# First norm's weight and bias: on VectorE ahead of the spill instead of mostly on GpSimd behind it; second gated unit's weights split ahead of that

## The chip, the cores and the metric

The kernel runs on one core of one Trainium2 chip. The metric is the device time of one execution in microseconds. Three runs of the kernel before give 1960.56, 1960.99 and 1962.79; the median is 1960.99.

## What is computed

One encoder layer over 1024 tokens of 1024 features in float32, with three sub-layers of the same outer form; a vector `c` gives each its shift, scale and gate. The last multiplication and addition of the layer norm, by `g` and `b`, are what the change moves, for the first sub-layer.

```python
def layer_norm(x, g, b):
    ...
    y = (xf - mu) * lax.rsqrt(var + LN_EPS)
    return (y * g.astype(jnp.float32) + b.astype(jnp.float32)).astype(x.dtype)

def post_norm_sublayer(x, mod, weight, f, g, b):
    shift, scale, gate = mod[:, 0, None, :], mod[:, 1, None, :], mod[:, 2, None, :]
    y = f(x * (1.0 + scale) + shift)
    return layer_norm(ALPHA * x + weight * (1.0 + gate) * y, g, b)

def swiglu(h, w_in, w_out):
    gate, up = jnp.split(h @ w_in, 2, axis=-1)
    return (jax.nn.silu(gate) * up) @ w_out

def hybrid_mixer(h, ...):
    proj = h @ w_in
    glu_a, glu_b, q, k, v = jnp.split(proj, ...)        # 512 columns each
    conv_out = conformer_conv(glu_a, glu_b, ...)        # u = glu_a * sigmoid(glu_b); depthwise, 31 wide; layer norm; silu
    attn_out = diff_attention(q, k, v, ...)             # two softmax maps per head, partial rotary on q and k
    return jnp.concatenate([conv_out, attn_out], axis=-1) @ w_out

    x = post_norm_sublayer(x, mod[:, 0], 0.5, swiglu 1, ln1_g, ln1_b)
    x = post_norm_sublayer(x, mod[:, 1], 1.0, hybrid_mixer, ln2_g, ln2_b)
    x = post_norm_sublayer(x, mod[:, 2], 0.5, swiglu 2, ln3_g, ln3_b)
```

## The kernel before

Tokens lie in eight tiles of 128 (`xt[t]`, one token per partition). Every matrix product is made from three: each operand is split into a rounded high part (a cast, `split`, L139, on ScalarE) and the rest (a subtraction, L140, on VectorE), and high by high, low by high and high by low are summed. The two SwiGLU products use the Strassen-Winograd form, with halves of the tokens and of the columns.

The stages follow each other in this way. SwiGLU 1 ends with `out_phase`, which calls `done(t)` for each finished token tile and `after(half, k)` for each feature tile of a half. `done` normalizes `xt[t]` without `g` and `b` (`norm_tile`, L257) and writes it to DRAM (`spill1[t]`, L883), from ScalarE's queue. `after` transposes the normalized tiles (`hT1`), and the mixer's features `hm` come from these with `g`, `b`, the shift and the scale folded into one scale and bias per feature (`A1`, `B1`): the mixer does not read `g` and `b` in token form. They are needed only in the residual of sub-layer 2.

The mixer's projections (pool `mproj`) come next. Four gated units of 128 columns each are made (`glu`, L913): unit `i` has weights loaded by `load_glu` in two halves (`glur`, from SP's queue), split into `gluh` and `glul`; `u` is the product of one part with the sigmoid of the other (`sg`, L920; `u`, L921). The weights of unit 0 are split early, in `done(4)`, into slots of a general heap. Then k, q and v are projected (`proj_tok`, L948 and L961), k and q get their rotary terms on GpSimd (L978 to L981). The depthwise convolution runs on VectorE (`cacc`, L926 and L932, 4 + 120 instructions), with a low priority, so that it fills the time between others. `ql` is the low part of the rotated queries (L1026 on VectorE, L1028 on GpSimd), transposed into `qT` by TensorE (L1040), and the scores (`sc`, L1055) follow, with their maxima on VectorE (`mx`, L1058).

After the attention of a tile, `finish(t)` scales it by the root of its squares' mean (`ss`, L1145, and a chain of small instructions on 128x4, L229 to L241, then L1149). The output projection (pool `p3a`) reads the normalized tiles back from DRAM into `x1[t]` (L1250, SP's queue), multiplies by `g` and adds `b` (`affine`, L266 and L267; tiles 0 to 5 on GpSimd, 6 and 7 on VectorE, by `XG`), and adds the products `mo` (L1293) of features `fh`, `fl` and weights `moh`, `mol` to it on VectorE (L1297 for the first quarter, L1299 behind it). What follows there is in an order given by a string (`MSEQ`).

The engines execute their own instructions in order. The order on each is made by a scheduler, from priorities that follow the code except where they are set by hand. SP's queue carries nearly all loads, in order: a DMA that waits keeps back all that stand behind it.

Of the kernel before, what the change touches and what calls it, by code (L numbers as in the profile page):

```python
# [17 lines left out]
NT = T // P  # L18
# [5 lines left out]
H = 512  # L24
# [12 lines left out]
XG = 6  # L37
# [13 lines left out]
def layer_kernel(ctx, tc, a, out):  # L51
# [227 lines left out]
    # Strassen-Winograd right operands of a pair of feature tiles (2 k, 2 k + 1); token halves are the columns.  # L279
    def right_first(name, ops, hb, eng=V):  # L280
        """hb: feature tiles 2 k and 2 k + 1 of token half 0."""
# [5 lines left out]
    def right_second(name, ops, hb, hc, eng=G, lo=V):  # L287
        """hc: feature tiles 2 k and 2 k + 1 of token half 1."""
# [35 lines left out]
    def in_tags(wp, order):  # L324
        """Has the tiles that are free first lie first."""
        for tag in order.split():
            shape, bufs = TAGS[tag]
            wp.tile(shape, F32, tag=tag, bufs=bufs, name=f"{tag}_")
# [43 lines left out]
    def product(ps, left, right, ks=range(4), more=False):  # L372
        """more: on top of the sum that the bank holds."""
# [11 lines left out]
    even = {}  # L385
# [6 lines left out]
    def in_steps(wp, s, j, L, ops, gd, begun={}):  # L392
        """The seven products of a pair of gate and up tiles; the left operands of the second half to DRAM."""
# [11 lines left out]
        def prod(left, right, ps=None):  # L405
            """ps: the bank that holds the sum so far."""
# [127 lines left out]
    # ---- SwiGLU, second half: product with w_out in Strassen-Winograd form (token halves, halves of the columns,  # L534
    # even and odd feature tiles), residual; done(t) follows each finished token tile; after(half, k) the tiles
    # of a half, some way into the next products ----
    def out_phase(s, wp, w_out, gd, gate, xs, done, after, hook):
# [6 lines left out]
        wa = {}  # L544
# [6 lines left out]
        def prep(n, k):  # L551
            """Operands of step k of product n; wa holds B11, then T1, and B22, wb B12, then T3, and B21, then T4."""
# [139 lines left out]
    # ================= sub-layer 1 =================  # L692
    x_in = a["x"][0]
    with pool("p1a") as wp:
# [27 lines left out]
        def first_mod(kk, raws, n):  # L722
            """The last n of its four blocks are summed on the vector engine first."""
# [47 lines left out]
        def early(wp, s, w_in, ops):  # L771
# [10 lines left out]
            # a: ada loads, x: token loads, w: weights, M: modulation, H: modulated features, R: right  # L782
            # operands, G and S: left operands, g: products; "d" has the vector engine take more of it
# [55 lines left out]
    with pool("p1b") as wp:  # L839
# [41 lines left out]
        def done(t):  # L881
            norm_tile(xt[t], f"1_{t}")
            S.dma_start(spill1[t], xt[t])  # L883
# [597 lines left out]
```

## Time and profile before

| | |
|---|---|
| median of three runs | 1960.99 us |
| span of the profiled execution (the page has no other time for it) | 1958.3 us |
| TensorE busy | 1832.7 us, 94% |
| VectorE busy | 1538.3 us, 79% |
| ScalarE busy | 781.3 us, 40% |
| GpSimd busy | 405.6 us, 21% |
| the twelve affine instructions on GpSimd | from 1131.65 to 1162.0 us |

The span is that of one execution; starts in the timelines are counted from its begin. Engines are named PE (TensorE matmuls), PEld (its weight loads), DVE (VectorE), ACT (ScalarE), POOL (GpSimd) and SP. Out and in of an instruction stand as `out<-in`, by the program's names without their numbers.

### The profile page before, as it was taken

Reading aid. Unit: us, or ns where it says so; the run is one execution under the profiler, and the core shown is the slowest. Engines: PE = TensorE matmul, PEld = TensorE weight load, DVE = VectorE, ACT = ScalarE, POOL = GpSimd, SP = SyncE. Lnnn points to the kernel's source line nnn. Section 1 sums busy time; section 2 is a strip of 40 time slices with the busy share of each in tenths; the row PEclk is TensorE's granted clock in tenths of the full one; section 3 lists DMA queues with packets and bytes.
Section 4 is the critical chain, followed back from the end, with each engine's and each line's share of the span. In section 5 each row is a group of like instructions: output and inputs, shape, how many; then the busy total and the mean of one; then the engine's idle time right before and its main releaser. Section 6 shows DMA issues by size and latency. Waiting matters only on the chain. (4 is left out here: it accounts for less than half of the span.)

```text
span 1958.3 us, 23453 instructions
## 1 busy us (share of the span) xinstructions
PE 1832.7 (94%) x8562; PEld 1514.4 (77%) x8562; DVE 1538.3 (79%) x2276; ACT 781.3 (40%) x1240; POOL 405.6 (21%) x280
## 2 busy tenths in 40 slices
PE   5899999999999999999999859989999999997896
PEld 4688888888888788888888748768888888885675
DVE  8867768675697978999689989896565756589888
ACT  3423333333445441142677642643333333443541
POOL 2200000000000020168476561430000000036034
PEclk7899999999999999999999879989999999998998
DMA  8527445533885322110000032234333432574511
GB/s 251 166 92 223 157 140 188 167 119 130 302 282 155 113 95 62 33 44 33 1 1 1 25 124 78 97 114 139 102 100 116 129 97 86 192 261 155 162 65 70
DMA packets 201394, 238.39 MB, mean 122 GB/s; under 512 B 13866, under 2 KB 124575, under 8 KB 201278
## 3 DMA queue, kind: packets, MB, share of 16 engines
q1 hardware_dynamic: 197786, 225.06, 35.7%
q0 software_dynamic: 2112, 7.34, 1.0%
q10 hardware_dynamic: 1380, 4.49, 0.6%
q8 instruction: 67, 1.10, 0.2%
q14 instruction: 49, 0.40, 0.1%
HBM read 183.89 MB, written 52.95 MB: 121 GB/s over the span
## 5 line engine op out<-in xcount | busy, mean ns | idle before, releaser
L589 PE MATMUL fo<-wr,gl 128*128 128x512 f32 x1848 | 430.4, 394 | 25.8 <-DVE wr L140 13.3
L589 PEld LDWEIGHTS fo<-wr,gl 128*128 128x128 f32 x1848 | 349.2, 190 | 105.0 <-DVE wr L140 16.0
L140 DVE TENSOR_TENSOR sl<-sf,sh 128x1024 fp32r<-128x1024 f32 x87 | 110.6, 1272 | 145.2 <-ACT sh L139 145.2
L139 ACT CAST sh<-sf 128x1024 fp32r<-128x1024 f32 x88 | 92.7, 1053 | 209.9 <-issue 31.5
L399 POOL DMA_DIRECT2D gd<-gf x8 | 4.5, 568 | 824.9 <-DVE gf L465 824.3
L932 DVE SCALAR_TENSOR_TENSOR cacc<-u,convw,cacc 128x1015 f32<-128x1015 f32 (+14 forms) x120 | 152.3, 1319 | 0.9
L140 DVE TENSOR_TENSOR gl<-gr,gl 128x512 fp32r<-128x512 f32 x148 | 110.6, 754 | 8.1 <-ACT gl L139 6.7
L139 ACT CAST gl<-gr 128x512 fp32r<-128x512 f32 x148 | 90.6, 618 | 64.1 <-DMA gr<-gd 56.2
L153 DVE SCALAR_TENSOR_TENSOR ada<-adaw,c_act,ada 128x512 f32<-128x512 f32 x98 | 73.3, 748 | 36.5 <-DMA adaw<-in_w_ada_dram 35.7
L266 POOL TENSOR_TENSOR x<-x,row_ln_g 128x1024 f32<-128x1024 f32 (+1 forms) x28 | 65.0, 2334 | 169.1 <-ACT x L257 100.8
L1058 DVE TENSOR_REDUCE mx<-sc 128x1 f32<-128x1024 f32 x64 | 76.1, 1216 | 19.8 <-PE sc L1056 19.8
L1060 ACT ACTIVATE p<-sc,mx 128x1024 f32<-128x1024 f32 x64 | 71.3, 1115 | 48.0 <-DVE mx L1058 46.7
L139 ACT CAST ah<-ra 128x1536 fp32r<-128x1536 f32 x44 | 65.0, 1478 | 58.6 <-DMA ra<-in_ffn_w_in_dram 14.4
L140 DVE TENSOR_TENSOR al<-ra,ah 128x1536 fp32r<-128x1536 f32 x44 | 77.1, 1751 | 1.2 <-ACT ah L139 1.2
L427 ACT ACTIVATE gf<-gf 128x512 f32<-128x512 f32 x44 | 27.8, 632 | 118.5 <-DVE gf L426 109.7
L140 DVE TENSOR_TENSOR wr<-wa,wr 128x512 fp32r<-128x512 f32 x66 | 54.1, 819 | 23.7 <-ACT wr L139 23.6
L1293 PE MATMUL mo<-moh,fh 128*128 128x512 f32 x128 | 51.3, 401 | 20.7 <-DVE x L1297 20.1
L139 ACT CAST wr<-wa 128x512 fp32r<-128x512 f32 x66 | 41.1, 622 | 62.4 <-PE fo L589 61.8
L913 PE MATMUL glu<-hm,gluh 128*128 128x512 f32 x256 | 65.7, 392 | 0.0
L1112 POOL TENSOR_TENSOR p<-p,p 128x1024 f32<-128x1024 f32 x27 | 64.8, 2401 | 1.9
L1129 PE MATMUL av<-vf,aT 128*128 128x128 f32 x512 | 62.7, 276 | 1.2 <-ACT cacc L1190 0.8
L139 ACT CAST wr<-wb 128x512 fp32r<-128x512 f32 x66 | 40.1, 620 | 55.3 <-PE fo L589 45.3
(3503 smaller groups left out, 4858.8 us busy)
## 6 DMA issues: line engine op xcount, KB each, us to landing
gr<-gd SPq DMA_DIRECT2D x148, 256.0 KB, 3.0
ra<-in_ffn_w_in_dram SPq DMA_DIRECT2D x132, 256.0 KB, 4.1
adaw<-in_w_ada_dram SPq DMA_DIRECT2D x56, 512.0 KB, 4.0
gd<-gf SPq DMA_DIRECT2D x102, 256.0 KB, 2.1
rb<-in_ffn_w_in_dram SPq DMA_DIRECT2D x44, 256.0 KB, 3.1
wb<-in_ffn_w_out_dram SPq DMA_DIRECT2D x44, 256.0 KB, 5.0
wa<-in_ffn_w_out_dram SPq DMA_DIRECT2D x44, 256.0 KB, 4.8
gd<-s SPq DMA_DIRECT2D x40, 256.0 KB, 4.2
```

The source lines that it names most:

```text
L139: a = S.copy(hi, x)
L140: b = eng.tensor_tensor(lo, x, hi.bitcast(F32), ALU.subtract)
L153: V.scalar_tensor_tensor(acc, raw[:, jj], c_act[:, n : n + 1], acc, ALU.mult, ALU.add)
L266: eng.tensor_tensor(x, x, g, ALU.mult)
L589: PE.matmul(ps, lhsT=g[:, x, ts_], rhs=w[:, y], start=n in (1, 2, 3) and k == i == 0, stop=k == NK - 1 and i == 2, skip_group_check=n not ...
L913: PE.matmul(q[2 * m + h], lhsT=w[:, m * P : (m + 1) * P], rhs=hm[k][h][:, x], start=k == 0 and n == 0, stop=k == KD - 1 and n == 2,)
L932: V.scalar_tensor_tensor(acc[:, lo_t:hi_t], u[:, lo_t + sh : hi_t + sh], convw[:, i, jj : jj + 1], acc[:, lo_t:hi_t], ALU.mult, ALU.add,)
L1058: V.tensor_reduce(mx_, ps, axis=AX.X, op=ALU.max, negate=True)
L1060: S.activation(pe, ps, AF.Exp, bias=mx_, accum_out=sm[:, e : e + 1])
L1112: last = G.tensor_tensor(p0, p0, p1, ALU.add)
L1129: PE.matmul(ps[:, 0:P], lhsT=aT[:, kt], rhs=vf[kt][:, h * P : (h + 1) * P], start=kt == 0, stop=kt == 7)
L1293: pe = PE.matmul(ps, lhsT=x[:, ts_], rhs=w[:, ds_], start=n == 0, stop=n == total - 1)
```

## The change

The multiplication by `g` and the addition of `b` are made in the pool of SwiGLU 1, behind its last `after`, for all eight tiles on VectorE, and the spill of each tile stands behind them, on SP's queue. Ahead of that the second gated unit's weights are loaded and split, into slots of the heap. In `p3a` the tiles read back are used as they are. The other lines of the diff take comments out, by which later lines move by one, or by up to three.

```diff
-XG = 6
...
         def done(t):
             norm_tile(xt[t], f"1_{t}")
-            S.dma_start(spill1[t], xt[t])
             if t == 4:
                 pre.extend(load_glu(wp, 0, None, None, 0, "ar", 2))
...
         out_phase(0, wp, a["ffn1_w_out"][0], gd, mods["gate0"], xs, done, after, hook)
+        pre2 = load_glu(wp, 1, None, None, 0, "ar", 2)
+        rows1 = row_bcast("ln1_g"), row_bcast("ln1_b")
+        for t in range(NT):
+            affine(xt[t], *rows1, V)
+            SY.dma_start(spill1[t], xt[t])
...
-            ws = pre if i == 0 else load_glu(wp, i, "whi", "wlo", 4, "raw", 3)
+            ws = (pre, pre2)[i] if i < 2 else load_glu(wp, i, "whi", "wlo", 4, "raw", 3)
...
         x1 = []
-        rows1 = row_bcast("ln1_g"), row_bcast("ln1_b")
         for t in range(NT):
             tag = ("sf", "sf", "sh", "sl", "sh", "sl", "sh", "sl")[t]
             x1.append(wp.tile([P, D], F32, tag=tag, bufs=TAGS[tag][1], name=f"x1_{t}"))
             SY.dma_start(x1[t], spill1[t])
-            affine(x1[t], *rows1, G if t < XG else V)
```

On VectorE, at the start of the projections, before: behind the last `hm` the halves of the weights of units 1 and 2 are split, then `u0` is formed and the convolution begins.

```order
L893 TENSOR_TENSOR hm71_5878<-h1_7_1_5876,hm71_5878 128x512
L140 TENSOR_TENSOR glul10_6001<-glur10_5997,gluh10_6000 128x1024
L140 TENSOR_TENSOR glul11_6008<-glur11_6004,gluh11_6007 128x1024
L140 TENSOR_TENSOR glul20_6122<-glur20_6118,gluh20_6121 128x1024
L140 TENSOR_TENSOR glul21_6129<-glur21_6125,gluh21_6128 128x1024
L921 TENSOR_TENSOR u0_5990<-sg0_0_5991,glu00_5892 128x512
L921 TENSOR_TENSOR u0_5990<-sg0_1_5994,glu00_5892 128x512
L926 TENSOR_SCALAR cacc_5888<-u0_5990,convw_89,vec_87 128x1024
L932 SCALAR_TENSOR_TENSOR cacc_5888<-u0_5990,convw_89,cacc_5888 128x1009
L932 SCALAR_TENSOR_TENSOR cacc_5888<-u0_5990,convw_89,cacc_5888 128x1010
```

The same place in the changed kernel, from the last two of the sixteen affine instructions (L265 and L266, on `x0_0` to `x0_7`), ahead of which the last `hm` and the two splits of unit 1 stand as before.

```order
L266 TENSOR_TENSOR x0_6_4966<-x0_6_4966,row_ln1_b_5889 128x1024
L266 TENSOR_TENSOR x0_7_5008<-x0_7_5008,row_ln1_b_5889 128x1024
L924 TENSOR_TENSOR u0_6024<-sg0_0_6025,glu00_5926 128x512
L924 TENSOR_TENSOR u0_6024<-sg0_1_6028,glu00_5926 128x512
L929 TENSOR_SCALAR cacc_5922<-u0_6024,convw_89,vec_87 128x1024
L935 SCALAR_TENSOR_TENSOR cacc_5922<-u0_6024,convw_89,cacc_5922 128x1009
L139 TENSOR_TENSOR glul20_6142<-glur20_6138,gluh20_6141 128x1024
L924 TENSOR_TENSOR u1_6131<-sg1_0_6132,glu10_6031 128x512
L924 TENSOR_TENSOR u1_6131<-sg1_1_6135,glu11_6032 128x512
L139 TENSOR_TENSOR glul21_6149<-glur21_6145,gluh21_6148 128x1024
L139 TENSOR_TENSOR glul30_6261<-glur30_6257,gluh30_6260 128x1024
L935 SCALAR_TENSOR_TENSOR cacc_5922<-u0_6024,convw_89,cacc_5922 128x1010
```

The sixteen stand ahead of `u0`, and the splits of unit 2 (`glul20`, `glul21`) have moved behind it, from ahead of it.

On SP before, at the same place: the loads of the four units' weights, and behind them those for k.

```order
L870 DMA glur11_6004<-in_mix_w_in_dram 128x4x128
L871 DMA glur11_6004<-in_mix_w_in_dram 128x4x128
L870 DMA glur20_6118<-in_mix_w_in_dram 128x4x128
L871 DMA glur20_6118<-in_mix_w_in_dram 128x4x128
L870 DMA glur21_6125<-in_mix_w_in_dram 128x4x128
L871 DMA glur21_6125<-in_mix_w_in_dram 128x4x128
L870 DMA glur30_6237<-in_mix_w_in_dram 128x4x128
L871 DMA glur30_6237<-in_mix_w_in_dram 128x4x128
L870 DMA glur31_6244<-in_mix_w_in_dram 128x4x128
L871 DMA glur31_6244<-in_mix_w_in_dram 128x4x128
L948 DMA kr0_6482<-in_mix_w_in_dram 128x2x512
```

On SP in the changed kernel: the two loads of the affine's rows and the eight spills, each of which waits for VectorE's addition of its tile, stand between the loads of units 1 and 2.

```order
L870 DMA glur11_5880<-in_mix_w_in_dram 128x4x128
L261 DMA row_ln1_g_5887<-in_ln1_g_dram 128x1024
L261 DMA row_ln1_b_5889<-in_ln1_b_dram 128x1024
L898 DMA spill1_0_3722<-x0_0_4210 128x1024
L898 DMA spill1_1_3723<-x0_1_4233 128x1024
L898 DMA spill1_2_3724<-x0_2_4256 128x1024
L898 DMA spill1_3_3725<-x0_3_4378 128x1024
L898 DMA spill1_4_3726<-x0_4_4860 128x1024
L898 DMA spill1_5_3727<-x0_5_4922 128x1024
L898 DMA spill1_6_3728<-x0_6_4966 128x1024
L898 DMA spill1_7_3729<-x0_7_5008 128x1024
L869 DMA glur20_6138<-in_mix_w_in_dram 128x4x128
```

The loads of unit 2 stand behind the spills, and those of unit 3 and of k behind them.

On VectorE before, at the end of the convolution: `ql0`, the low part of the first rotated queries, stands behind all 124 instructions of it, and the first maxima follow.

```order
L932 SCALAR_TENSOR_TENSOR cacc_5888<-u3_6351,convw_89,cacc_5888 128x1013
L932 SCALAR_TENSOR_TENSOR cacc_5888<-u3_6351,convw_89,cacc_5888 128x1012
L932 SCALAR_TENSOR_TENSOR cacc_5888<-u3_6351,convw_89,cacc_5888 128x1011
L932 SCALAR_TENSOR_TENSOR cacc_5888<-u3_6351,convw_89,cacc_5888 128x1010
L932 SCALAR_TENSOR_TENSOR cacc_5888<-u3_6351,convw_89,cacc_5888 128x1009
L1026 TENSOR_TENSOR ql0_7368<-qf0_7030,qh0_7367 128x8x64
L1058 TENSOR_REDUCE mx00_7427<-sc00_7422 128x1
L1058 TENSOR_REDUCE mx01_7436<-sc01_7431 128x1
```

The same place in the changed kernel.

```order
L935 SCALAR_TENSOR_TENSOR cacc_5922<-u2_6250,convw_89,cacc_5922 128x1011
L935 SCALAR_TENSOR_TENSOR cacc_5922<-u3_6371,convw_89,cacc_5922 128x1016
L1029 TENSOR_TENSOR ql0_7388<-qf0_7050,qh0_7387 128x8x64
L935 SCALAR_TENSOR_TENSOR cacc_5922<-u2_6250,convw_89,cacc_5922 128x1010
L935 SCALAR_TENSOR_TENSOR cacc_5922<-u3_6371,convw_89,cacc_5922 128x1015
L935 SCALAR_TENSOR_TENSOR cacc_5922<-u2_6250,convw_89,cacc_5922 128x1009
L935 SCALAR_TENSOR_TENSOR cacc_5922<-u3_6371,convw_89,cacc_5922 128x1014
L935 SCALAR_TENSOR_TENSOR cacc_5922<-u3_6371,convw_89,cacc_5922 128x1013
L935 SCALAR_TENSOR_TENSOR cacc_5922<-u3_6371,convw_89,cacc_5922 128x1012
L935 SCALAR_TENSOR_TENSOR cacc_5922<-u3_6371,convw_89,cacc_5922 128x1011
L935 SCALAR_TENSOR_TENSOR cacc_5922<-u3_6371,convw_89,cacc_5922 128x1010
L935 SCALAR_TENSOR_TENSOR cacc_5922<-u3_6371,convw_89,cacc_5922 128x1009
```

Nine instructions of the convolution have come to stand behind `ql0`, and the first maxima follow them. Of the 124, 45 stood before ahead of the product `u3` and 31 do now.

On GpSimd the twelve rows of L266 and L267 are gone (259 rows against 271); VectorE has sixteen more and four less (2252 against 2240).

## Rows read from the trace of the kernel before

**Rows 1.** The page's first part: busy us (share of the span) xinstructions:

```profile
PE 1832.7 (94%) x8562; PEld 1514.4 (77%) x8562; DVE 1538.3 (79%) x2276; ACT 781.3 (40%) x1240; POOL 405.6 (21%) x280
```

**Rows 2.** Waits of TensorE: what for, us in total, times, longest:

```profile
PE mo L1293 <- DVE x L1297: 20.1, 1, 20.1
```

**Rows 3.** Timeline of TensorE, 1140 to 1170: start, us, [idle before]:

```profile
1140.21 0.50 PE L1293 MATMUL mo<-moh,fh 128*128 128x512 f32 x1
...
1145.56 0.39 PE L1293 MATMUL mo<-moh,fl 128*128 128x512 f32 x1
1166.08 0.79 PE L1293 MATMUL mo<-moh,fh 128*128 128x512 f32 x1 [20.13 <-DVE x L1297]
...
1169.19 0.39 PE L1293 MATMUL mo<-mol,fh 128*128 128x512 f32 x1
```

**Rows 4.** Windows: stretch, us, busy of each engine, granted clock, DMA, GB/s:

```profile
737.00:803.00 66.00, 66.00 (x293) 54.66 (x292) 63.47 (x57) 10.31 (x13) 0.00 (x0) 1.00 0.17 50
803.00:925.00 122.00, 120.53 (x571) 100.24 (x570) 119.30 (x101) 35.75 (x73) 78.04 (x66) 1.00 0.11 35
1146.00:1166.00 20.00, 0.00 (x0) 0.00 (x0) 19.66 (x15) 0.66 (x1) 15.93 (x7) 0.57 0.10 39
1166.00:1170.00 4.00, 3.92 (x11) 3.15 (x12) 4.00 (x6) 0.00 (x0) 0.00 (x0) 0.61 0.00 0
```

**Rows 5.** Timeline of VectorE, 1140 to 1167:

```profile
1140.96 2.37 DVE L1145 TENSOR_SCALAR ss<-ss 128x4 f32<-128x4 f32 x1
...
1148.16 2.26 DVE L237 TENSOR_TENSOR nt_o<-nt_o,ss 128x4 f32<-128x4 f32 x1
...
1165.34 1.28 DVE L1297 SCALAR_TENSOR_TENSOR x<-x,mo 128x512 f32<-128x512 f32 x2
```

**Rows 6.** Timeline of GpSimd, 1159 to 1163: the last affine:

```profile
1159.66 2.34 POOL L267 TENSOR_TENSOR x<-x,row_ln_b 128x1024 f32<-128x1024 f32 x1
```

**Rows 7.** Timeline of VectorE, 1129 to 1131: the chain of the tile before:

```profile
1130.17 0.16 DVE L237 TENSOR_TENSOR nt_o<-nt_o,ss 128x4 f32<-128x4 f32 x1
1130.36 0.17 DVE L239 SCALAR_TENSOR_TENSOR nz_o<-nt_o,nz_o 128x4 f32<-128x4 f32 x1
```

**Rows 8.** Timeline of ScalarE, 1138 to 1146:

```profile
1138.59 0.23 ACT L1139 ACTIVATION_READ_ACCUMULATOR sq<-o 128x1 f32 x1
...
1142.67 2.11 ACT L139 CAST moh<-mor 128x1024 fp32r<-128x1024 f32 x2
```

**Rows 9.** Timeline of VectorE, 1172 to 1173: an affine beside idle GpSimd:

```profile
1172.59 1.22 DVE L266 TENSOR_TENSOR x<-x,row_ln_g 128x1024 f32<-128x1024 f32 x1
```

**Rows 10.** Timeline of VectorE, 729 to 762: start of the projections:

```profile
729.25 3.49 DVE L140 TENSOR_TENSOR glul<-glur,gluh 128x1024 fp32r<-128x1024 f32 x3
736.93 1.23 DVE L140 TENSOR_TENSOR glul<-glur,gluh 128x1024 fp32r<-128x1024 f32 x1 [4.20 <-ACT gluh L139]
738.84 1.29 DVE L921 TENSOR_TENSOR u<-sg,glu 128x512 f32<-128x512 f32 x2 [0.68 <-ACT sg L920]
...
760.43 1.28 DVE L921 TENSOR_TENSOR u<-sg,glu 128x512 f32<-128x512 f32 x2
```

**Rows 11.** The page's DMA view: issues, KB each, median us to landing:

```profile
x<-spill SPq DMA_DIRECT2D x16, 512.0 KB, 8.2
...
glur<-in_mix_w_in_dram SPq DMA_DIRECT2D x16, 256.0 KB, 4.0
```

**Rows 12.** Timeline of VectorE, 917 to 938: end of the convolution:

```profile
917.11 8.36 DVE L932 SCALAR_TENSOR_TENSOR cacc<-u,convw,cacc 128x1014 f32<-128x1014 f32 x6
925.38 0.69 DVE L1026 TENSOR_TENSOR ql<-qf,qh 128x512 fp32r<-128x512 f32 x1
935.56 2.36 DVE L1058 TENSOR_REDUCE mx<-sc 128x1 f32<-128x1024 f32 x2 [9.49 <-PE sc L1056]
```

**Rows 13.** Timeline of all engines, 926 to 928:

```profile
926.15 0.62 POOL L1028 TENSOR_SCALAR ql<-ql 128x512 fp32r<-128x512 f32 x1 [5.67 <-DVE ql L1026]
...
927.65 0.50 PE L1040 MATMUL qTl<-ident_r,ql 128*128 128x128 f32 x4
```

## The prediction

> **What bounds the kernel now.** I read the busy shares first: TensorE works 94% of the span [rows 1], so what another engine saves counts only where TensorE waits. The page gives the profiled execution's span, 1958.3 us, and no time of its own beside it; the runs shown have a median of 1960.99, so some 2.7 us lie around the span, and I carry every difference over to that median. Next I read TensorE's waits, longest first: the longest of the whole kernel, 20.1 us in one piece, stands at the output projection's matmuls, L1293, which wait for VectorE's L1297 [rows 2]. TensorE's timeline there shows 24 matmuls up to 1145.56, the next one only at 1166.08, and a slower pace behind it [rows 3]. VectorE is not idle in that stretch (19.66 of 20 us busy [rows 4]), so I read its timeline. Ahead of L1297 it goes through the square-root chain of the last attention tile, thirteen instructions on 128x4, nine of which show 2.2 to 2.4 us (two of the nine: [rows 5]); meanwhile GpSimd runs its twelve affine instructions, the last until 1162.0 [rows 6]. The same chain of the tile before, with GpSimd idle, shows 0.16 us an instruction and one every 0.2 us [rows 7]. A 128x4 instruction that lasts as long as one GpSimd instruction is being held by it; nothing in the chain reads the affine's data.
>
> **Part 1: twelve GpSimd and four VectorE instructions leave the output projection.** Without GpSimd's work the stretch runs as follows. The first two `fl` splits (1.22 each, as a free instruction of this shape [rows 9]) are through when the tile's squares are summed on ScalarE at 1138.8 [rows 8]. Thirteen steps of 0.2 and one 128x512 product of 0.7 end at about 1142.1. `mol` of two weight tiles is next and now waits for their casts on ScalarE, 2.11 us from 1142.67 [rows 8]: the second cast ends at 1144.8, its `mol` of 1.22 at 1146.0, the first L1297 of 0.7 at 1146.7. So what is late next is ScalarE's cast, and TensorE goes on at about 1146.8, where it could have at 1145.9: 0.9 of the 20.1 stays, 19.2 go. [...] Gain 20.7. The loads that this stage waits for next (`ra`, behind the later `fl`) move up with it. The four VectorE instructions (1.22 each [rows 9]) stand between L1297s that TensorE did not wait for; I cost them at nothing, and if that is wrong they give up to 4.9.
>
> [...]
>
> **Part 2: sixteen affine instructions enter VectorE at the start of the mixer's projections.** There VectorE splits three weight halves from 729.25, idles 4.20 before the next split and 0.68 before `u0` [rows 10], and from then on hardly waits: 63.47 of 66 us busy, then 119.30 of 122; TensorE is at 66.00 and 120.53 there, GpSimd at 0.00 and 78.04 [rows 4]. So the new work meets some 6 us of holes (66 - 63.47 and what precedes 737) and a convolution of 124 instructions as a buffer behind. Sixteen instructions at the pace of three splits of the same shape, (3.49 - 1.22)/2 = 1.135 [rows 9, 10], take 18.2: from 731.5 to 749.7. Behind them wait `u0` (749.8 instead of 738.84), a few of the convolution, then the third unit's weight split, whose loads now stand on SP's queue behind the eight spills, each of which waits for its affine. With issue at 750.3, 4.0 to land [rows 11], a cast of 1.06 (half of 2.11 [rows 8]) and a split of 1.22 these are ready at 757. TensorE turns to that unit shortly before `u1` is formed at 760.43 [rows 10], at about 759: 2 us of margin, no stall. With the 8.2 that the spills' reads took [rows 11] the stall would be 2.5; I take 0, since 4.0 is the row of these very loads, and keep 2.5 as the upper end.
>
> [...]
>
> The load of VectorE is carried on as convolution not yet done. By the order, 45 of the 124 convolution instructions stand ahead of the fourth unit's product before and 31 now; VectorE reaches that product with TensorE's pace either way. The scheduler then puts the first query split, `ql0` (L1026), ahead of the last 9 convolutions, where it stood behind all 124. So at `ql0` VectorE is 14 - 9 = 5 instructions later: at the pace of the last six, 8.27/6 = 1.38 [rows 12], 6.9 us, so 932.3 instead of 925.38. GpSimd's copy (0.62) then ends at 933.7, where it ended at 926.77, and TensorE's `qTl` transposes started at 927.65: 0.88 of slack [rows 13]. TensorE stands still for 6.9 - 0.9 = 6.0. Bounds: 0, if the convolution is less late than counted, and 17.3, if all 18.2 are carried here. The 9 convolutions behind `ql0` (12 us) lie in the 9.49 that VectorE waits before its first maximum [rows 12], now some 6 longer, so they cost nothing more; without that cover they would cost 3. A stall lowers the clock, as the one of 20 us did [rows 3, 4]; this one is shorter, and I take the same 1.5 (bounds 0 and twice that). What starts late here stays late: the attention is one chain from `qT` on.
>
> **Part 3: small moves.** About 715 to 730 the order of TensorE puts transposes of the last features, which wait for ScalarE, ahead of matmuls that stood before them. No row prices this; the nearest wait is that of `u0` for ScalarE, 0.68 [rows 10]. I take 1.0, bounds 0 and two such waits, 1.4. ScalarE, busy 40% [rows 1], issues eight spills less, and the affine's two rows are loaded early into free slots: nothing.
>
> **Sum.** 1960.99 - 20.7 + 6.0 + 1.5 + 1.0 = 1948.8.
>
> **Rivals.** A: the backlog is covered. VectorE's idle in part 2 takes all of it, or `ql0` finds TensorE later anyway; for it speaks that the queues meet within a few us, against it VectorE's 119.30 of 122 [rows 4]. Then only part 3 remains: 1960.99 - 20.7 + 1.0 = 1941.3. B: the backlog is not covered at all; TensorE's and VectorE's full 188 us speak for it [rows 4], the order's 9 convolutions behind `ql0` against: 1960.99 - 20.7 + 17.3 + 1.5 + 1.0 = 1960.1, no change. C, on the other side: the 20 us at L1293 stay. The chain would be slow there for itself, and GpSimd's instructions only beside it; then nothing is gained and 8.5 is paid, 1969.5. It decides once less than 8.5 of the gap goes. Against it stands the same chain at 0.16 [rows 7]. That the change does not do what it says is ruled out by the order: GpSimd has 12 rows less, VectorE 12 more net.
>
> **How the numbers follow.** The forecast, with its own range 1944 to 1954 (qTl between 2 and 9, landing 0 to 2.5), has 0.66, A 0.14, B 0.15, C 0.05. The range reaches into A and towards B: 1941 to 1957. A measurement can tell about 0.2%, 3.9 us. Faster by more than that: the forecast, A and a fifth of B, 0.83; within it 0.12; slower 0.05.
>
> **What would show it.** In the changed profile: the wait at L1293 about 1 us and behind a `mol`, 128x4 instructions at 0.16 everywhere, the granted clock near 1.00 behind it; sixteen 128x1024 instructions of 1.2 us on VectorE from about 731 to 750; no wait of L913 for `gluh`; a new wait of about 6 us of TensorE for GpSimd's `ql` near 928. It is wrong if the chain's instructions still take 2 us, if the glu matmuls wait, or if that wait is 0 or 17 us.

## The result, and the profile after

The changed kernel takes 1949.22 us (median of 4 runs, 1948.52 to 1950.04), the kernel before on the same chip 1961.14 (4 runs, 1960.56 to 1962.79): a ratio of 0.9944, 95% interval 0.9930 to 0.9957. The profiled execution has a span of 1947.5 against 1958.3, and a mean granted clock of 0.976 against 0.968. Of all runs in this document one, of e6 below, was in a slow state (6441.9 us): the ratios leave it out, and e6's median in the table counts it (1956.92 without it).

A span of 10.8 less is made of one large gain and several small losses. The starts of TensorE's stages, counted from the span's begin in each trace, show where they arise:

| first matmul of | gated units | k | v | scores | output projection (`mo`) |
|---|---|---|---|---|---|
| before | 711.0 | 802.9 | 897.4 | 934.5 | 1140.2 |
| after | 710.9 | 804.2 | 900.4 | 944.0 | 1150.0 |

The output projection begins 9.8 later than before, and the kernel ends 10.8 earlier. The large gain lies behind the output projection's start: from there to the end it is 797.5 us, where it was 818.1, 20.6 less. The losses lie between 711 and 944.

TensorE's waits in the changed kernel from 705 to 1230 (what for, us in total, times, longest) no longer hold the 20.1 of [rows 2], of which the last line is what is left. Those for `qh` and `ql` are new; the one for `khl` was there before, with 1.5.

```profile
PE qTh L1043 <- POOL qh L1030: 2.8, 1, 2.8
...
PE kT L1007 <- DVE khl L139: 1.7, 1, 1.7
...
PE qTl L1043 <- POOL ql L1031: 1.5, 1, 1.5
...
PE mo L1294 <- DVE x L1298: 1.0, 1, 1.0
```

**The gap.** TensorE's timeline where [rows 3] had its hole:

```profile
1155.37 0.39 PE L1294 MATMUL mo<-moh,fl 128*128 128x512 f32 x1
1156.74 0.50 PE L1294 MATMUL mo<-moh,fh 128*128 128x512 f32 x1 [0.98 <-DVE x L1298]
1157.08 0.40 PE L1294 MATMUL mo<-mol,fh 128*128 128x512 f32 x1
```

The matmul behind the first 24 now waits 0.98 us, not 20.13, and the matmuls from 1157.08 on start 0.23 apart, not 0.44. VectorE's timeline there answers to [rows 5]:

```profile
1148.65 0.17 DVE L1148 TENSOR_SCALAR ss<-ss 128x4 f32<-128x4 f32 x1 [0.22 <-ACT sq L1142]
1148.86 0.17 DVE L228 TENSOR_SCALAR nz_o<-ss 128x4 int32<-128x4 int32 x1
...
1151.03 0.17 DVE L240 TENSOR_SCALAR r<-nz_o 128x4 f32<-128x4 f32 x1
...
1153.73 2.36 DVE L139 TENSOR_TENSOR mol<-mor,moh 128x1024 fp32r<-128x1024 f32 x2 [1.80 <-ACT moh L138]
1156.01 1.27 DVE L1298 SCALAR_TENSOR_TENSOR x<-x,mo 128x512 f32<-128x512 f32 x2
```

And ScalarE's at the same time, which answers to [rows 8]:

```profile
1150.47 2.22 ACT L1157 ACTIVATE featA<-oT,sub_g 128x128 f32<-128x128 f32 x8
1152.47 2.10 ACT L138 CAST moh<-mor 128x1024 fp32r<-128x1024 f32 x2
```

All thirteen chain instructions take 0.16 or 0.17. Then VectorE idles 1.80 for the casts of `moh`, splits two `mol`, and makes the first L1298: what is late next is ScalarE's cast, as forecast.

**The start of the projections.** VectorE's timeline, which answers to [rows 10]:

```profile
731.71 2.35 DVE L265 TENSOR_TENSOR x<-x,row_ln_g 128x1024 f32<-128x1024 f32 x2
...
747.61 2.35 DVE L266 TENSOR_TENSOR x<-x,row_ln_b 128x1024 f32<-128x1024 f32 x2
749.88 1.27 DVE L924 TENSOR_TENSOR u<-sg,glu 128x512 f32<-128x512 f32 x2
...
752.04 1.27 DVE L935 SCALAR_TENSOR_TENSOR cacc<-u,convw,cacc 128x1009 f32<-128x1009 f32 x1
756.20 1.23 DVE L139 TENSOR_TENSOR glul<-glur,gluh 128x1024 fp32r<-128x1024 f32 x1 [2.89 <-ACT gluh L138]
761.27 1.28 DVE L924 TENSOR_TENSOR u<-sg,glu 128x512 f32<-128x512 f32 x2 [3.85 <-ACT sg L923]
```

The sixteen affine instructions, in pairs, fill 731.71 to 749.88. The split of the third unit is through at 757.4, and no `glu` matmul waits for it. But VectorE then stands idle 2.89 and 3.85 us ahead of `u1`, since the order leaves only two convolution instructions there. Two rows of the page's DMA view answer to [rows 11] (the last number is the median of the landings that the profile recorded, which are few):

```profile
glur<-in_mix_w_in_dram SPq DMA_DIRECT2D x16, 256.0 KB, 3.7
spill<-x SPq DMA_DIRECT2D x8, 512.0 KB, 2.6
```

The 3.7 is not the time behind the spills. It is the middle of two recorded landings: 2.98 for a load issued at 696.24, long ahead of them, and 4.41 for one issued at 751.99, behind them. Before, the row's 4.0 stands between 2.98 and 5.05. So one load behind the spills is on record, and it took 4.4.

**The queries.** TensorE's timeline where the queries are transposed ([rows 13]):

```profile
930.13 0.39 PE L964 MATMUL vp<-vh,hm 128*128 128x512 f32 x1
933.31 0.74 PE L1043 MATMUL qTh<-ident_r,qh 128*128 128x128 f32 x4 [2.79 <-POOL qh L1030]
935.51 0.75 PE L1043 MATMUL qTl<-ident_r,ql 128*128 128x128 f32 x4 [1.45 <-POOL ql L1031]
...
943.97 0.39 PE L1058 MATMUL sc<-kst,qTh 128*128 128x512 f32 x1
```

VectorE's where the convolution ends ([rows 12]):

```profile
914.54 17.23 DVE L935 SCALAR_TENSOR_TENSOR cacc<-u,convw,cacc 128x1022 f32<-128x1022 f32 x13
932.71 1.08 DVE L1029 TENSOR_TENSOR ql<-qf,qh 128x512 fp32r<-128x512 f32 x1 [0.93 <-POOL qh L1028]
```

GpSimd's, from the first rotary product of the queries to the last of `ql0`:

```profile
878.19 12.80 POOL L981 TENSOR_TENSOR rcq<-qf,ropec 128x128 f32<-128x128 f32 x1 [11.13 <-ACT qf L1013]
890.96 1.30 POOL L982 TENSOR_TENSOR rsq<-qf,ropec 128x64 f32<-128x64 f32 x1
...
932.06 0.61 POOL L1028 TENSOR_SCALAR qh<-qf 128x512 fp32r<-128x512 f32 x1
...
933.88 1.58 POOL L1031 TENSOR_SCALAR ql<-ql 128x512 fp32r<-128x512 f32 x1 [0.62 <-DVE ql L1029]
```

The first rotary product in the kernel before:

```profile
875.18 0.92 POOL L978 TENSOR_TENSOR rcq<-qf,ropec 128x128 f32<-128x128 f32 x1 [7.91 <-ACT qf L1010]
```

GpSimd's in e1 (the kernel before without the affine, below):

```profile
877.64 12.40 POOL L978 TENSOR_TENSOR rcq<-qf,ropec 128x128 f32<-128x128 f32 x1 [9.47 <-ACT qf L1010]
...
925.59 0.33 POOL L979 TENSOR_TENSOR rsq<-qf,ropec 128x64 f32<-128x64 f32 x1
...
926.70 0.62 POOL L1025 TENSOR_SCALAR qh<-qf 128x512 fp32r<-128x512 f32 x1
```

Two engines are late at the same time. VectorE's convolution ahead of `ql0` ends at 931.77, near the 932.3 of the forecast. GpSimd still works on the rotary terms of the queries until 932.06, so that `qh`, which before was ready some 7 us ahead of its use, is late too. TensorE waits 2.79 for it and 1.45 for `ql`. GpSimd's first rotary product, begun at 878.19, took 12.80 us where it took 0.92 before, but that alone does not make `qh` late: in e1 it took 12.40, and TensorE did not wait for `qh`. Beside the convolution these GpSimd instructions take 1.28 to 1.45 each (1.30 in the second row above). In e1 VectorE is through with the convolution at 924.49, and the last five of them ahead of `qh` take 0.32 to 0.46; in the changed kernel the convolution goes on until 931.77, and none of them is that short. So it is the held product and the longer convolution together; without the hold (e9 below) the wait for `qh` is gone. From the v product ahead of the transposes to the first scores TensorE now needs 943.97 - 930.13 = 13.84 us; before it was 934.46 - 927.12 = 7.34. Of the 6.5 more, 4.2 are the two waits; the other 2.3 go with the lower clock (third window below).

The windows of the three stretches (stretch, us, busy of PE, PEld, DVE, ACT, POOL, granted clock, DMA, GB/s); the second answers to the last two of [rows 4]:

```profile
711.00:737.00 26.00, 24.60 (x121) 19.13 (x120) 18.43 (x33) 13.98 (x16) 8.82 (x12) 1.00 0.08 32
1150.00:1160.00 10.00, 9.01 (x38) 7.13 (x39) 7.96 (x16) 6.46 (x13) 0.00 (x0) 1.00 0.71 254
933.00:944.00 11.00, 9.24 (x41) 7.64 (x42) 10.86 (x9) 2.27 (x4) 6.45 (x5) 0.69 0.01 1
```

Between 711 and 737 TensorE is busy 24.60 us, where before it was 25.60 in the same stretch: the moved transposes wait for ScalarE. Behind the gap the clock is 1.00, no longer 0.57 and 0.61; it is 0.69 around and behind the new waits at 933.

**The clock between k and v.** From the first k matmul to the first v matmul TensorE takes 96.25 us, where it took 94.51 before. The same window in the traces of before, of the changed kernel and of e1, with the columns as above:

```profile
861.00:865.00 4.00, 4.00 (x19) 3.26 (x18) 4.00 (x4) 1.61 (x5) 4.00 (x4) 1.00 0.11 40
861.00:865.00 4.00, 4.00 (x21) 3.49 (x21) 4.00 (x4) 2.82 (x9) 3.99 (x4) 0.57 0.47 131
861.00:865.00 4.00, 4.00 (x16) 3.29 (x16) 4.00 (x4) 2.52 (x8) 3.92 (x4) 0.57 0.29 103
```

Behind its wait for `khl` (1.47 us in before, 1.72 in the changed kernel, 1.47 in e1) TensorE's granted clock over these four us is 0.57 in the last two and 1.00 in the first (in the changed kernel it is 0.50 from 861.4 to 864.8, 3.4 us); over the whole stretch it is 0.982 against 1.000, and 1.8% of 96.25 us is 1.7. e1, whose order there is that of before, takes 96.05 us, so that this loss is not the change's.

### The profile page after: what moved, and what is told of

Same layout as the page of the kernel before. It is cut to its first block, busy times and chain, and to the rows that moved or that the text cites. A ratio compares the mean times of both kernels' runs of the same rounds, so it can differ in the third digit from the quotient of the medians.

```text
span 1947.5 us, 23459 instructions
## 1 busy us (share of the span) xinstructions
PE 1837.9 (94%) x8562; PEld 1518.5 (78%) x8562; DVE 1527.6 (78%) x2288; ACT 782.0 (40%) x1240; POOL 386.9 (20%) x268
## 3 DMA queue, kind: packets, MB, share of 16 engines
q0 software_dynamic: 2112, 7.34, 1.0%
## 5 line engine op out<-in xcount | busy, mean ns | idle before, releaser
L935 DVE SCALAR_TENSOR_TENSOR cacc<-u,convw,cacc 128x1019 f32<-128x1019 f32 (+13 forms) x120 | 151.7, 1324 | 0.2
L265 POOL TENSOR_TENSOR x<-x,row_ln_g 128x512 f32<-128x512 f32 (+1 forms) x22 | 50.4, 2305 | 159.4 <-ACT x L256 100.6
L1058 PE MATMUL sc<-kst,qTh 128*128 128x512 f32 x128 | 56.2, 439 | 6.0 <-ACT p L1063 5.6
```

The lines of the kernel that those rows point to most:

```text
L265: eng.tensor_tensor(x, x, g, ALU.mult)
L935: V.scalar_tensor_tensor(acc[:, lo_t:hi_t], u[:, lo_t + sh : hi_t + sh], convw[:, i, jj : jj + 1], acc[:, lo_t:hi_t], ALU.mult, ALU.add,)
L1058: PE.matmul(ps[:, ks], lhsT=qTh[:, m], rhs=kst[m][:, ks], start=True, stop=False)
```

## Experiments

Every kernel below was timed beside the kernel before on the same chip. "Qk" is the time from the first `glu` matmul to the first scores, of the profiled execution, in which the affine's load has to be worked off: 223.4 us before, 233.1 after.

| run | what it is | Qk, us | median, us | ratio to before (95%) |
|---|---|---|---|---|
| e1 | before, no affine at all | 224.9 | 1940.01 | 0.9893 (0.9876-0.9909) |
| e2 | after, no affine at all | 226.7 | 1942.33 | 0.9909 (0.9895-0.9924) |
| e3 | after, affine on GpSimd | 254.3 | 1971.58 | 1.0057 (1.0042-1.0071) |
| e4 | after, six tiles early, two late | 232.9 | 1949.26 | 0.9942 (0.9927-0.9956) |
| e5 | after, order written out | 239.4 | 1954.42 | 0.9969 (0.9956-0.9982) |
| e6 | e5 with six tiles early | 239.9 | 1957.07 | 0.9976 (0.9967-0.9986) |
| e7 | before, affine all on VectorE | 223.3 | 1960.64 | 0.9998 (0.9988-1.0007) |
| e8 | after, no early split of unit 1 | 243.2 | 1961.48 | 0.9996 (0.9987-1.0005) |
| e9 | after, GpSimd let in early | 233.5 | 1950.64 | 0.9950 (0.9933-0.9967) |
| e10 | after, holes filled | 231.6 | 1947.14 | 0.9932 (0.9917-0.9947) |
| e11 | e10 with six tiles early | 233.2 | 1949.98 | 0.9947 (0.9932-0.9961) |
| e12 | e10, fewer convolution instructions ahead of k and q | 229.0 | 1945.86 | 0.9924 (0.9910-0.9938) |

### The terms taken apart: e1, e2

```diff
 # e1, from the kernel before
-        rows1 = row_bcast("ln1_g"), row_bcast("ln1_b")
...
-            affine(x1[t], *rows1, G if t < XG else V)
 # e2, from the changed kernel
-        rows1 = row_bcast("ln1_g"), row_bcast("ln1_b")
...
-            affine(xt[t], *rows1, V)
```

> The kernel before without the multiplication by g and the addition of b in the output projection (left out altogether, with the two loads of their rows; what is read back from the spill is used as it is). Theory (GpSimd's long instructions hold VectorE's 128x4 chain, one each): the wait of 20.1 us at L1293 shrinks to about 1.0, the clock stays near 1.00 behind it, nothing else moves: 1961.1 - 19.1 - 1.5 = 1940.5, between 1939.5 and 1942. Rival (the chain is slow there for itself): the 128x4 instructions keep their 2.3 us, the wait stays near 20, about 1961.

> The changed kernel without the sixteen affine instructions and the two loads of their rows (the spill on SP's queue behind the norm and the early split of unit 1 stay). Theory (the loss of 9.8 us on TensorE up to the output projection is VectorE's backlog): the first scores come at about 936 instead of 944.0, no wait for qh or ql, only the 1.3 us of the stretch 711 to 737 stay: 1940.5 + 1.3 = 1941.8, between 1940 and 1943.5. Rival (the loss comes from the spills on SP's queue and from the new order of TensorE and of the weight splits): first scores stay at about 944, 1948 to 1949.5.

e1 came out at 1940.01 and e2 at 1942.33, both in their ranges. In e1, with nothing else changed, the wait at L1291 is what it is in the changed kernel, and the thirteen chain instructions take 0.16 or 0.17, the one of 2.37 in [rows 5] too. The wait, and that instruction in VectorE's timeline:

```profile
PE mo L1291 <- DVE x L1295: 1.0, 1, 1.0
```

```profile
1141.35 0.17 DVE L1145 TENSOR_SCALAR ss<-ss 128x4 f32<-128x4 f32 x1 [0.22 <-ACT sq L1139]
```

So the three steps are measured apart: taking the affine from the place it had, 1940.01 - 1961.07 = -21.1; moving the early split and the spills, 1942.33 - 1940.01 = +2.3, which the intervals of the two ratios do not keep clear of noise; sixteen instructions on VectorE at the new place, 1949.22 - 1942.33 = +6.9. In e2 neither `qh` nor `ql` is waited for, so that the waits at the queries belong to the sixteen instructions.

### Where the affine may stand: e7, e3

```diff
 # e7, from the kernel before
-XG = 6
+XG = 0
 # e3, from the changed kernel
-            affine(xt[t], *rows1, V)
+            affine(xt[t], *rows1, G)
```

> The kernel before with all eight tiles' affine on VectorE behind the spill (XG = 0), nothing moved ahead of it. Theory: no GpSimd instruction runs beside the 128x4 chain, so that takes 0.16 an instruction, but fifteen of the sixteen instructions stand in VectorE's order ahead of the first L1297: 15 x 1.135 = 17.0 and the 1.0 that stays, a wait of 16 to 18.5 us at L1293 with the same low clock behind it: 1957.5, between 1955 and 1960. [...]

> The changed kernel with the affine at its new place on GpSimd instead of VectorE, where GpSimd was idle from 730 to 825. Theory (each GpSimd instruction of 2.34 us holds VectorE for as long): sixteen of them cost VectorE about 16 x 2.3 = 37 us less the idle it has there, more than the 18.2 on VectorE itself; its 128x1024 instructions between 731 and 775 take up to 3.5, and the first scores come later than 944: 1950 to 1968, most likely 1956. Rival (GpSimd is idle there, so the work is free): first scores at about 936, 1941 to 1943.

e7: the time is that of before, just above the range, and the wait within its range:

```profile
PE mo L1293 <- DVE x L1297: 18.2, 1, 18.2
```

GpSimd is free there and the chain is no longer held (0.16 or 0.17 an instruction), and yet 18.2 of the 20.1 us remain, because fifteen of the sixteen instructions now stand on VectorE ahead of the first L1297, from 1146.92 to 1164.07. Freeing the chain is not enough; the work had to leave the stretch.

e3: slower, as expected, but by more than its range. VectorE's timeline of e3:

```profile
731.93 6.75 DVE L139 TENSOR_TENSOR glul<-glur,gluh 128x1024 fp32r<-128x1024 f32 x2
...
743.88 3.28 DVE L935 SCALAR_TENSOR_TENSOR cacc<-u,convw,cacc 128x1009 f32<-128x1009 f32 x1
776.65 1.23 DVE L139 TENSOR_TENSOR glul<-glur,gluh 128x1024 fp32r<-128x1024 f32 x1 [29.50 <-ACT gluh L138]
```

And TensorE's:

```profile
776.67 0.79 PE L916 MATMUL glu<-hm,gluh 128*128 128x512 f32 x1 [15.52 <-ACT gluh L138]
```

Beside GpSimd's affine (729 to 770) two splits take 6.75 us, not 2.35, and a convolution instruction 3.28, not 1.27. The size that was underestimated is SP's queue: the last spill waits for GpSimd, the loads of the third unit stand behind it and are issued from 770.75 on, and TensorE waits 15.52 us for them.

### The early split: e8

```diff
-        pre2 = load_glu(wp, 1, None, None, 0, "ar", 2)
...
-            ws = (pre, pre2)[i] if i < 2 else load_glu(wp, i, "whi", "wlo", 4, "raw", 3)
+            ws = pre if i == 0 else load_glu(wp, i, "whi", "wlo", 4, "raw", 3)
```

> The changed kernel without the early load and split of unit 1's weights, which then stand behind the spills on SP's queue like those of units 2 and 3. Theory (the loads wait for the spills, and these for the affine until 750): TensorE needs unit 1 at about 737 and gets it at 757: a wait of 18 to 21 us at the glu matmuls, of which VectorE's backlog gains back what it owed (no wait for qh and ql): 1949.2 + 20 - 5 = 1964, between 1960 and 1970. Rival (the loads pass the spills or are hidden): within 2 us of the changed kernel.

1961.48, in the range; the wait is 14.81, under the 18 to 21 that were expected. TensorE's timeline of e8:

```profile
753.53 3.78 PE L915 MATMUL glu<-hm,gluh 128*128 128x512 f32 x8 [14.81 <-ACT gluh L138]
```

Without that edit the second unit's loads stand behind eight spills that wait for VectorE, and the whole gain is lost. The early split costs at most the 2.3 of e2 - e1, and without it 10 us are lost by the ratios to the kernel before, 12 by the medians.

### Less load, and another order: e4, e5, e6

```diff
 # e4, from the changed kernel; e6 has the same
-            affine(xt[t], *rows1, V)
+            if t < 6:
+                affine(xt[t], *rows1, V)
...
+        rows2 = row_bcast("ln1_g"), row_bcast("ln1_b")
...
+            if t >= 6:
+                affine(x1[t], *rows2, V)
```

> The changed kernel with tiles 0 to 5 at the new place and tiles 6 and 7 behind the spill on VectorE, where they were before. Theory (each early affine costs TensorE about as much as VectorE): four of the sixteen less, 4.5 us of VectorE, so the first scores come 3 to 4.5 earlier, and the four cost nothing in the output projection: 1945.5, between 1944 and 1947.5. Rival (what is late at the scores is GpSimd's rotary work and not the count of VectorE's instructions): 1948.5 to 1950.

It missed, and the rival's number held: 4.5 us of VectorE work less, and no time won. VectorE's timeline of e4 at the start:

```profile
754.72 1.23 DVE L139 TENSOR_TENSOR glul<-glur,gluh 128x1024 fp32r<-128x1024 f32 x1 [5.92 <-ACT gluh L138]
```

VectorE's at the queries:

```profile
932.75 1.08 DVE L1030 TENSOR_TENSOR ql<-qf,qh 128x512 fp32r<-128x512 f32 x1 [0.93 <-POOL qh L1029]
```

GpSimd's there:

```profile
932.10 0.62 POOL L1029 TENSOR_SCALAR qh<-qf 128x512 fp32r<-128x512 f32 x1
```

At the start the 4.5 us became idle time ahead of the third unit's split (5.92 where it was 2.89). And at the queries GpSimd ends its rotary terms at 932.10, as in the changed kernel (932.06), with VectorE's `ql0` waiting for it. There are two bounds, and this edit lowered neither. The two tiles that went back cost nothing at the output projection: from its first matmul to the end e4 takes 797.6 us, the changed kernel 797.5.

The next two write the convolution's order out: how many of the 124 instructions precede each named step, 7 of them ahead of `u1` in e5 and 10 in e6, where the changed kernel has 2.

```diff
 # e5; e6 has other numbers
+        UPTO = {'w2': 5, 'u1': 7, 'u2': 21, 'u3': 36, 'k0': 53, 'k2': 60, 'k4': 69, 'k6': 76, 'v0': 92, 'v1': 96, 'v2': 99, 'v3': 103, 'q': 115, 'end': 124}
...
+            for n in range(nconv[0], UPTO[name]):
+                i, m = divmod(n, 31)
```

> The changed kernel with VectorE's order written out in the projections: 7 instead of 2 instructions of the convolution ahead of u1, 21 instead of 16 ahead of u2, 36 instead of 31 ahead of u3, 5 more ahead of the first khl, 4 to 6 ahead of the others; 115 ahead of ql0 as now. Theory (six of VectorE's idle us stand in front of u1, because the order leaves them empty, and the backlog at ql0 is those): u1 without a wait, ql0 some 5 us earlier on VectorE, the waits of TensorE for qh and ql go down from 4.3 us to below 2, first scores between 938 and 941: 1944, between 1942 and 1946.5. Rival (GpSimd's rotary work, held by VectorE for 12 us near 878, ends at 932 whatever VectorE has done): qh still late, first scores 943 to 944, 1948 to 1950.

> The same written-out order with tiles 0 to 5 early and tiles 6 and 7 behind the spill on VectorE (10 instructions of the convolution ahead of u1, 25 ahead of u2, 40 ahead of u3, 119 ahead of ql0). Theory: the 4.5 us that the four instructions less left as a hole in front of u1 are filled here, so this is the one where six tiles are worth something: no wait for qh and ql beyond 1, first scores 937 to 940, 1942.5, between 1941 and 1945.5. Rival (GpSimd's rotary work decides): 1948 to 1950.

Both missed, and their medians are 5 and 8 us over the changed kernel's. VectorE's timeline of e5:

```profile
772.61 1.23 DVE L140 TENSOR_TENSOR kl<-kr,kh 128x1024 fp32r<-128x1024 f32 x1 [4.68 <-ACT kh L139]
773.75 10.50 DVE L925 SCALAR_TENSOR_TENSOR cacc<-u,convw,cacc 128x1017 f32<-128x1017 f32 x8
```

The same place in the changed kernel:

```profile
773.66 9.56 DVE L935 SCALAR_TENSOR_TENSOR cacc<-u,convw,cacc 128x1014 f32<-128x1014 f32 x8
```

Eight convolution instructions take 10.50 us, not 9.56: this order goes through one accumulator after the other, and instructions that add to the same one start 1.30 apart, not 1.19. It also opened a hole of 4.68 ahead of `kl`. So `ql0` came at 938.49, later than the 932.71 it was to improve. As a test of the holes e5 and e6 were spoiled by these two.

### Which of the two late engines: e9

From here on the written order alternates between accumulators, except for some fifteen instructions around GpSimd's first rotary product, which stay on one. e9 keeps the changed kernel's numbers of instructions ahead of each step.

```diff
+            if not (len(convs) in [73, 74, 75, 76, 77, 78, 79, 80, 81, 82, 83, 84, 85, 86] and todo[last[0]]):
+                free = [i for i in free if i != last[0]] or free
```

> The changed kernel in the same order on every engine, but of the convolution's instructions between the last khl and the first vl (73rd to 87th) all fifteen go to one accumulator, where the changed kernel alternates two tiles; consecutive instructions on one accumulator start 1.30 apart instead of 1.19, with a small pause between. Theory (without a pause VectorE keeps GpSimd's first rotary product of q waiting for 12 us; with pauses GpSimd gets in): no GpSimd instruction longer than 2.5 us, GpSimd's rotary work ends some 10 us earlier (near 921 instead of 932), no wait of TensorE for qh; VectorE, slower by 2 to 3 us in those fifteen, is then alone late, so ql0 and the wait for ql stay: first scores 943 to 946, 1948.5 to 1951.5. Rival (GpSimd's end is what held everything, VectorE would have been early): first scores 939 to 941, 1944 to 1946.

1950.64, in the range. GpSimd's timeline of e9 at the first rotary product:

```profile
880.65 1.47 POOL L1005 TENSOR_TENSOR rcq<-qf,ropec 128x128 f32<-128x128 f32 x1 [12.55 <-ACT qf L1038]
```

TensorE's at the queries:

```profile
937.46 0.54 PE L1072 MATMUL qTl<-ident_r,ql 128*128 128x128 f32 x4 [4.18 <-POOL ql L1060]
```

GpSimd got in (1.47, not 12.80), and TensorE no longer waits for `qh`. It waits 4.18 for `ql` alone, as long as for both together in the changed kernel (4.24). But VectorE pays for it: the fifteen instructions take 20.02 us where the changed kernel's take 17.90, and its convolution ahead of `ql0` ends 223.1 us behind the first `glu` matmul, not 220.9. Most of that is not the one accumulator's: in the trace of before, where GpSimd got in beside alternating accumulators, the convolution instructions from 875.70 to 887.70 start 1.33 apart as well, and those of e9 behind GpSimd's entry 1.35. While GpSimd is held, VectorE runs at 1.19; letting it in costs VectorE about what the changed kernel had won by the hold. So by itself it wins nothing; that VectorE's lateness alone would have cost the 4.2 is not shown by it.

### The holes filled: e10, e11, e12

```diff
 # e10: 5 and 7 instructions ahead of the third unit's split and of u1 instead of 2 and 2
+        UPTO = {'w2': 5, 'u1': 7, 'u2': 21, 'u3': 36, 'k0': 53, 'k2': 60, 'k4': 68, 'k6': 77, 'v0': 92, 'v1': 96, 'v2': 100, 'v3': 104, 'q': 116, 'end': 124}
...
 # e12
+        UPTO = {'w2': 5, 'u1': 7, 'u2': 20, 'u3': 34, 'k0': 50, 'k2': 57, 'k4': 65, 'k6': 74, 'v0': 90, 'v1': 94, 'v2': 98, 'v3': 102, 'q': 114, 'end': 124}
```

The lines of e9 are in all three, with the fifteen instructions at later places. e11 is e10 with six tiles early and two late, and its own numbers.

> The changed kernel with five more instructions of the convolution ahead of u1 and of everything behind it (7 ahead of u1, 21 ahead of u2, 36 ahead of u3, 53 ahead of the first khl, 92 ahead of the first vl, 116 ahead of ql0), alternating between two tiles as the changed kernel does, and the fifteen of e9 on one accumulator. Theory (both engines that were late, VectorE by the empty 6 us ahead of u1 and GpSimd by its 12 us, are earlier): ql0 at 927 to 930 on VectorE, waits of TensorE for qh and ql together below 2, first scores 938 to 941: 1945, between 1943 and 1947.5. Rival (the time is lost elsewhere again, by VectorE waiting for casts as in e5): 1949 or more.

> As e10, with tiles 0 to 5 early and 6 and 7 behind the spill on VectorE (9 instructions of the convolution ahead of u1, 56 ahead of the first khl, 117 ahead of ql0). Theory: VectorE is three instructions of the convolution further on than in e10, ql0 at 924 to 927, first scores 936 to 939: 1943.5, between 1941.5 and 1946. Rival: as in e4, no gain from the four instructions, within 1 us of e10.

> As e10 (all eight tiles early, the empty time ahead of u1 filled, fifteen instructions on one accumulator behind the last khl), with only two more instructions of the convolution than the changed kernel ahead of the first khl (50), 65 ahead of khl4, so that it stands ahead of the last split of the q weights, for whose cast VectorE waited 4.0 us in e10, and 114 ahead of ql0. Theory: TensorE's waits for khl fall from 5.2 to about 2.5, ql0 starts 4 to 6 us earlier than in e10 (928 to 930), waits for qh and ql below 1.5, first scores 938 to 941: 1944.5, between 1943 and 1947. Rival (VectorE's whole load up to the scores sets the time, whatever the order): first scores at 943 to 944 as in e10, 1946.5 to 1948.5.

e10 and e12 came within their ranges, e10 not by the way expected: its first scores are at 943.6, not 938 to 941, since TensorE waits 5.2 for `khl`. e11 missed: from the first k to the first v matmul it takes 102.9 us, e10 100.2. TensorE waits 6.0 for `khl` there, and its clock is 0.95, in e10 0.98. TensorE's waits in e12, from 705 to 1230:

```profile
PE kT L1032 <- DVE khl L140: 2.5, 3, 1.9
...
PE qTl L1072 <- POOL ql L1060: 1.1, 1, 1.1
```

With VectorE's idle time ahead of `u1` used and GpSimd let in, 1.1 us are left of the waits at the queries. The median is 3.4 under the changed kernel's; the intervals of the two ratios overlap (0.9910 to 0.9938 against 0.9930 to 0.9957), so that e12 is probably, not surely, the fastest of the kernels that do the whole work. Filling the idle time alone, without letting GpSimd in, in the alternating order, was not run, so that the shares of the two are not known. To e2 (1942.33), which has no affine at all, 3.5 us remain.

## Why the prediction was right

The forecast was 1948.8, the measured median 1949.22. The main mechanism and its size held. That the whole agrees to 0.4 us is luck: of the losses, one term was too large, two were too small or left out, and they nearly cancel.

- **The gap at the output projection (20.7 forecast).** Measured 21.1 by e1, and 20.6 in the traces (818.1 to 797.5). The step held in each part: GpSimd's instructions held the 128x4 chain, the next thing late was ScalarE's cast (0.98 left, 0.9 forecast), and the clock behind it came back. The 1.5 for the clock in the 20.7, and the same again at the queries, are the author's estimates, which no run shows by itself; the traces show seven matmuls behind the hole that start 0.44 apart before (granted clock 0.61) and 0.23 after (1.00), 7 x 0.21 = 1.5, and 2.3 at the queries. That the work had to leave the stretch, not only GpSimd, is shown by e7, and that the four VectorE instructions there cost nothing, as assumed, by e4.
- **Rival C (the chain slow for itself).** The rival would have left the chain at 2 us an instruction; it runs at 0.17. Nor are its first two, L1145 and L229 (2.37 and 2.33 us in before), slow for a reason of their own: L1148 and L228 in the changed kernel, the same two, take 0.17, so that they too were held by GpSimd.
- **Third unit's weights (ready at 757, no stall).** Ready at 757.4 and no stall. The one landing on record of a load behind the spills took 4.41, near the 4.0 of the forecast and not the 8.2 of its upper end. What SP's queue can cost is shown by e3 and e8: it waits for the data of a spill and holds back the loads behind it, 15.5 and 14.8 us. The upper end of 2.5 does not follow from its own terms: 750.3 + 8.2 + 1.06 + 1.22 = 760.8 is 1.8 behind 759.
- **The queries (6.0 + 1.5).** The whole is near, 6.5 in the trace and 6.9 by after - e2, but not its parts: the waits are 4.2, and 2.3 go with the clock. Two steps were off, in opposite directions. The working let TensorE come to `qTl` when it did before, and it came 3.0 later (first v product 900.4 against 897.4), which takes 3.0 from the wait. And it let GpSimd's copy of `ql0` end at 933.7, where it ends at 935.5: `ql0` had to wait 0.93 for `qh`, which the working had on time, and the copy took 1.58 beside the nine convolution instructions behind `ql0`, not 0.62, so that these were not free. That gives back 1.8; of the 4.8 that result, 4.2 show as waits. VectorE reached `ql0` near the forecast (931.77 against 932.3), in part by luck: while GpSimd's product is held it is faster (in e1, held, its convolution ends 212.5 us behind the first `glu` matmul; in before, not held, 214.5).
- **Rivals A and B.** A (covered, 1941.3) would have needed the load worked off before the queries. VectorE's idle time ahead of `u1`, 2.89 + 3.85, was not used for that; e12, which uses it and lets GpSimd in, has a median 3.4 lower. B (17.3 carried whole) did not occur either.
- **Small moves (1.0).** 1.4 in the trace (gated units to the first k matmul 91.9 before, 93.3 after). e1 has 91.9 and e2 93.3, so that these 1.4 come with the early split and the moved spills and not with the affine; the 2.3 of e2 - e1 is not clear of noise. The nearest row was too short, and the upper bound, 1.4, was just reached.
- **The stretch from k to v, not in the forecast.** It is 1.7 longer than before, by the lower clock (0.982 against 1.000), and e1 has it without the change. The kernel before has one profile, without that fall; how often its other executions have it is not known.

## What to carry to other kernels

Look at a chain of tiny instructions that each last as long as one instruction of another engine: here the 128x4 ones took up to 2.37 us beside GpSimd's of 2.34, and 0.16 or 0.17 without them (e1). Moving GpSimd's work off the stretch was worth nearly the whole wait (e1, 1.0 of 20.1 us left), moving it onto the held engine was not (e7, 18.2 left). Before counting a load as carried to the end, look for the idle time the order itself leaves behind a moved block, since lighter work there only lengthened it here (e4, 5.92 us idle instead of 2.89), and put ready work there (e12, whose gain is not clear of noise). When stores that wait for data move into a queue of loads, what stands behind them must be wanted late or be brought forward, as the early split was (without it TensorE waits 14.81 us, e8).

## What the runs showed of the hardware

- VectorE's convolution kept one GpSimd product waiting 12.80 us in the changed kernel, 11.7 to 12.8 in e1 to e4: it went on across some eleven of the convolution's instructions, which start 1.19 apart and take 1.27. In all five it got in behind the split `vl`, the first VectorE instruction of another kind. In e9, with 1.30 between the starts, it took 1.47, and in e12 0.46. In the profiles of before, e7 and e8 it took 0.92 to 0.98 beside alternating accumulators. Those are the three of the eight in which TensorE's clock did not fall between k and v (the longest `kT` matmul is 0.279 to 0.284 us there, 0.313 to 0.368 in the other five); whether the one brings the other is open.
- Once GpSimd is in, the two go on side by side: in the kernel before, convolution instructions start 1.33 apart, not 1.19, and most of GpSimd's rotary instructions take 1.28 to 1.45, not the 0.32 to 0.46 that they take in e1 when VectorE is through.
- VectorE instructions that add to the same accumulator start 1.30 apart, those that alternate 1.19: 10.50 us for eight in e5, 9.56 in the changed kernel.
- TensorE's clock fell behind a wait of 1.47 us in e1 (granted 0.57 over 861 to 865) and did not behind the same wait in the kernel before (1.00), nor behind one of 2.18 in e8 (no `kT` matmul over 0.284 us there, in e1 up to 0.313).
- The spills on SP's queue have one recorded landing each in three traces, 2.60 to 2.62 us (changed kernel, e3, e8); on ScalarE's queue, before, two are on record, 4.08 and 4.14. That the queue makes the difference is not shown.
